# A row mean of 64 MiB: hand-held semaphores, and each load in two halves of 64 partitions on two queues

## The chip, the cores and the metric

The kernel runs on one core of one Trainium2 chip. The metric is the device time of one execution in microseconds (us). The times given are medians of several runs; the profile is of one further execution, taken by the hardware profiler.

## The reference

The input is a 32 x 512 x 1024 array of float32, 64 MiB. Negative elements become zero, and each row of 1024 is averaged:

```python
def reference(x):
    relu_x = np.maximum(x, 0)
    return np.mean(relu_x, axis=-1).astype(np.float32)
```

The output has 32 x 512 float32 elements, 64 KiB.

## The kernel before

The 16,384 rows are spread over the 128 partitions: partition p holds rows p·128 to p·128+127, so J is 128 rows per partition, and each partition's part of the input is contiguous. The kernel walks over J in tiles of NB = 16 rows per partition. A full tile is 128 x 16 x 1024 float32, 8.39 MB, loaded by one DMA that SyncE (SP in the profile) issues on line 97. There are seven full tiles, in a pool of three buffers: the load of tile t+3 goes into the buffer of tile t and so waits until both engines that read tile t are done.

The eighth tile is loaded in pieces that get smaller towards the end, all issued by SyncE: 8, 4, 2 and 1 rows per partition (line 105), and the last row, in a buffer of its own called `last`, in columns of 512, 256 and 256 (line 109).

Each row of a tile is one instruction that takes the maximum with zero and sums along the row. Even rows go to ScalarE (ACT), by `act_row` on line 15; odd rows to VectorE (DVE), by `dve_row` on line 20. Both write over the tile and put the sum into a column of `sums`. GpSimd (POOL) multiplies the sums by 1/1024 into `res` (`finish`, line 90): once for the seven full tiles, once for the first 14 rows of the eighth. The last row but one is shared between ScalarE (448 columns) and VectorE (576), and GpSimd adds both parts (line 121). The last row is shared too: ScalarE sums 512 columns and VectorE 256, into two extra columns of `last`; then one VectorE instruction on line 126 multiplies the remaining 256 columns and those two partial sums by `scale` (filled with 1/1024 on line 81) and sums them into the last column of `res`. SyncE stores `res` by one DMA (line 130).

The order on each engine is the order in which the program is written. A tile framework derives the semaphores and waits from the buffers, hands its semaphores for DMAs out in turn, and on closing (line 134) adds drains, a meeting of all engines, a clear of its semaphores and a second meeting. After that, `issue_ahead_of_entry_barrier` moves SyncE's first load in front of the barrier at the program's entry, which the launching code adds (line 150 in the profile).

Of the kernel before, what the change touches and what calls it, by code (L numbers as in the profile page):

```python
# [1 line left out]

# [4 lines left out]

F32 = mybir.dt.float32
ALU = mybir.AluOpType
ACT = mybir.ActivationFunctionType  # L10


def act_row(nc, src, acc):

    nc.scalar.activation(out=src, in_=src, func=ACT.Relu, accum_out=acc)  # L15


def dve_row(nc, src, acc, init=None):

    nc.vector.tensor_scalar(  # L20
        out=src, in0=src, scalar1=0.0, scalar2=init,
        op0=ALU.max, op1=ALU.add, accum_out=acc,
    )


def issue_ahead_of_entry_barrier(nc):


    entry, body = nc.cur_f.blocks[0].instructions, None
    for block in nc.cur_f.blocks[1:]:  # L30
        for k, ins in enumerate(block.instructions):
            if ins.opcode == "DMACopy":
                body, load = block.instructions, k
                break
        if body is not None:
            break
    first = body[load]
    assert first.engine == mybir.EngineType.SP and not first.sync_info.on_wait
    assert all(i.opcode == "DMACopy" or i.engine != first.engine for i in body[:load])
    del body[load]  # L40
    at = next(k for k, i in enumerate(entry) if i.engine == first.engine and i.opcode == "Drain")
    entry.insert(at, first)


@with_exitstack
def kernel(
    ctx: ExitStack,
    tc: tile.TileContext,
    x: bass.AP,
    out: bass.AP,  # L50
):
    nc = tc.nc
    P = nc.NUM_PARTITIONS
    xf = x.flatten_outer_dims()
    R, D = xf.shape
    assert R % P == 0
    J = R // P
    inv = 1.0 / D
    xr = xf.rearrange("(p j) d -> p j d", p=P, j=J)
    outr = out.flatten().rearrange("(p j) -> p j", p=P, j=J)  # L60
    xlast = xr[:, J - 1, :]

    NB = 16
    full = J // NB - 1

    row_pieces = [8, 4, 2, 1]
    assert sum(row_pieces) == NB - 1
    col_pieces = [512, 256, 256]
    assert sum(col_pieces) == D

    pools = ctx.enter_context(ExitStack())
    in_pool = pools.enter_context(tc.tile_pool(name="in", bufs=3))
    res_pool = pools.enter_context(tc.tile_pool(name="res", bufs=1))
    sums = res_pool.tile([P, J], F32)
    res = res_pool.tile([P, J], F32)
    part = res_pool.tile([P, 2], F32)


    last = res_pool.tile([P, D + 2], F32)
    scale = res_pool.tile([P, D // 4 + 2], F32)  # L80
    nc.gpsimd.memset(scale, inv)  # L81

    def rows(xt, lo, n, j0):

        for k in range(lo, lo + n):
            j = j0 + k
            (dve_row if j % 2 else act_row)(nc, xt[:, k, :], sums[:, j:j + 1])

    def finish(lo, hi):
        nc.gpsimd.tensor_scalar(  # L90
            out=res[:, lo:hi], in0=sums[:, lo:hi], scalar1=inv, scalar2=0.0, op0=ALU.mult, op1=ALU.add,
        )

    for t in range(full):
        j0 = t * NB
        xt = in_pool.tile([P, NB, D], F32, name="xt")
        nc.sync.dma_start(out=xt, in_=xr[:, j0:j0 + NB, :])  # L97
        rows(xt, 0, NB, j0)

    j0 = full * NB  # L100
    xt = in_pool.tile([P, NB, D], F32, name="xt")
    prev = xt[:, NB - 2, :]
    lo = 0
    for n in row_pieces:
        nc.sync.dma_start(out=xt[:, lo:lo + n, :], in_=xr[:, j0 + lo:j0 + lo + n, :])  # L105
        lo += n
    c = 0
    for w in col_pieces:
        nc.sync.dma_start(out=last[:, c:c + w], in_=xlast[:, c:c + w])  # L109
        c += w  # L110

    finish(0, j0)
    lo = 0
    for n in row_pieces[:-1]:
        rows(xt, lo, n, j0)
        lo += n
    finish(j0, j0 + lo)

    act_row(nc, prev[:, :448], part[:, 0:1])
    dve_row(nc, prev[:, 448:], part[:, 1:2])  # L120
    nc.gpsimd.tensor_scalar(  # L121
        out=res[:, J - 2:J - 1], in0=part[:, 0:1], scalar1=part[:, 1:2], scalar2=inv, op0=ALU.add, op1=ALU.mult,
    )
    act_row(nc, last[:, :512], last[:, D:D + 1])
    dve_row(nc, last[:, 512:768], last[:, D + 1:D + 2])
    nc.vector.scalar_tensor_tensor(  # L126
        out=last[:, 768:], in0=last[:, 768:], scalar=0.0, in1=scale, op0=ALU.max, op1=ALU.mult,
        accum_out=res[:, J - 1:J],
    )
    nc.sync.dma_start(out=outr, in_=res)  # L130

    pools.close()
    tc.close()
    tc.compile()  # L134
    issue_ahead_of_entry_barrier(nc)


# [1 line left out]
_INS = ['x']  # L139
_OUTS = [((32, 512), 'float32')]  # L140


# [23 lines left out]
```

## Time and profile before

| | |
|---|---|
| median of 8 runs | 163.72 us (163.32 to 164.02) |
| profiled execution | 163.39 us, of which the span of its instructions is 161.6 us |
| bytes read, written | 67.11 MB, 0.07 MB |
| VectorE busy | 74.3 us |
| ScalarE busy | 69.2 us |
| one row of 1024 on VectorE, on ScalarE | 1208 ns, 1035 ns |

The span runs from the first to the last instruction of the core. "Busy" leaves out the sequencer's work: waits, semaphores and the issue of DMAs; such work has a "q" behind the engine's name (SPq). A line `A <- B: total, times, longest` in a view of waits says how long A waited for B. In the views by window the columns are the stretch, its length, busy time and instructions of VectorE, ScalarE and GpSimd, the granted TensorE clock (not used here), the busy share of 16 DMA engines, and GB/s.

### The profile page before, as it was taken

Reading aid. Unit: us, or ns where it says so; the run is one execution under the profiler, and the core shown is the slowest. Engines: PE = TensorE matmul, PEld = TensorE weight load, DVE = VectorE, ACT = ScalarE, POOL = GpSimd, SP = SyncE. Lnnn points to the kernel's source line nnn. Section 1 sums busy time; section 2 is a strip of 40 time slices with the busy share of each in tenths; the row PEclk is TensorE's granted clock in tenths of the full one; section 3 lists DMA queues with packets and bytes.
Section 4 is the critical chain, followed back from the end, with each engine's and each line's share of the span. In section 5 each row is a group of like instructions: output and inputs, shape, how many; then the busy total and the mean of one; then the engine's idle time right before and its main releaser. Section 6 shows DMA issues by size and latency. Waiting matters only on the chain.

```text
span 161.6 us, 351 instructions
## 1 busy us (share of the span) xinstructions
DVE 74.3 (46%) x132; ACT 69.2 (43%) x131; POOL 1.3 (1%) x8
## 2 busy tenths in 40 slices
DVE  0000049800696008940099202990049800698992
ACT  3000049600694008920099002980049600696882
POOL 1000000000000000000000000000000000000000
DMA  8997997997997997997997998998998996999990
GB/s 308 470 503 308 487 487 324 487 503 324 470 503 308 487 503 308 487 503 308 487 503 328 470 470 357 470 487 357 454 503 357 438 519 300 430 430 406 408 359 21
DMA packets 2162, 67.19 MB, mean 416 GB/s; under 512 B 240, under 2 KB 624, under 8 KB 880
## 3 DMA queue, kind: packets, MB, share of 16 engines
q1 hardware_dynamic: 2160, 67.18, 96.9%
q14 instruction: 2, 0.02, 0.0%
HBM read 67.11 MB, written 0.07 MB: 416 GB/s over the span
## 4 chain that ended last, share of the span: by engine, by line
DMA 84%; DVE 12%; SPq 1%; issue 0%; DVEq 0%
DMA xt<-in_x_dram 56%; DMA last<-in_x_dram 29%; DVE xt L20 11%; SPq L105 1%; SPq L109 0%; DVE last L20 0%; DVE last L126 0%; DVEq L126 0%; DVEq L20 0%; SPq L97 0%; DVEq L134 0%
## 5 line engine op out<-in xcount | busy, mean ns | idle before, releaser
L20 DVE TENSOR_SCALAR_CACHE_REDUCE xt<-xt 128x1024 f32<-128x1024 f32 x64 | 73.4, 1208 | 84.4 <-DMA xt<-in_x_dram 84.0
L15 ACT ACTIVATE xt<-xt 128x1024 f32<-128x1024 f32 x64 | 66.2, 1035 | 88.5 <-DMA xt<-in_x_dram 88.5
L15 ACT ACTIVATION_READ_ACCUMULATOR xt<-xt 128x1 f32 x64 | 11.9, 186 | 0.0
L20 DVE DVE_READ_ACCUMULATOR xt<-xt 128x1 f32 x64 | 5.3, 82 | 0.0
L90 POOL TENSOR_SCALAR res<-sums 128x112 f32<-128x112 f32 (+1 forms) x2 | 0.5, 249 | 155.8 <-DVE xt L20 155.8
L15 ACT ACT_TABLE_LOAD x1 | 1.3, 1283 | 0.8 <-PEq L150 0.8
L15 ACT ACTIVATE last<-last 128x512 f32<-128x512 f32 x1 | 0.6, 630 | 0.0
L126 DVE SCALAR_TENSOR_TENSOR last<-last,scale 128x258 f32<-128x258 f32 x1 | 0.4, 428 | 0.2 <-ACT last L15 0.2
L20 DVE TENSOR_SCALAR_CACHE_REDUCE last<-last 128x256 f32<-128x256 f32 x1 | 0.4, 419 | 0.2 <-DMA last<-in_x_dram 0.2
L81 POOL MEMSET scale<- 128x258 f32 x1 | 0.3, 314 | 0.3 <-POOLq L150 0.3
L121 POOL TENSOR_SCALAR res<-part 128x1 f32<-128x1 f32 x1 | 0.3, 264 | 0.7 <-DVE xt L20 0.7
L15 ACT ACTIVATION_READ_ACCUMULATOR last<-last 128x1 f32 x1 | 0.2, 187 | 0.0
L150 POOL MEMSET const-bfloat16-1.0<- 128x1 bf16 x1 | 0.1, 101 | 0.0
L150 POOL MEMSET const-uint8-127<- 128x1 uint8 x1 | 0.1, 101 | 0.0
L150 POOL MEMSET const-float32-0.0<- 128x1 f32 x1 | 0.1, 98 | 0.2 <-issue 0.2
L150 POOL MEMSET const-float32-1.0<- 128x1 f32 x1 | 0.1, 98 | 0.0
L126 DVE DVE_READ_ACCUMULATOR last<-last,scale 128x1 f32 x1 | 0.1, 83 | 0.0
L20 DVE DVE_READ_ACCUMULATOR last<-last 128x1 f32 x1 | 0.1, 82 | 0.0
## 6 DMA issues: line engine op xcount, KB each, us to landing
xt<-in_x_dram SPq DMA_DIRECT2D x1, 4096.0 KB, 39.0
xt<-in_x_dram SPq DMA_DIRECT2D x1, 2048.0 KB, 43.5
xt<-in_x_dram SPq DMA_DIRECT2D x1, 1024.0 KB, 45.5
xt<-in_x_dram SPq DMA_DIRECT2D x1, 512.0 KB, 46.4
last<-in_x_dram SPq DMA_DIRECT2D x1, 256.0 KB, 46.6
last<-in_x_dram SPq DMA_DIRECT2D x2, 128.0 KB, 42.7
xt<-in_x_dram SPq DMA_DIRECT2D x7, 48.7
out_dram<-res SPq DMA_DIRECT2D x1, 64.0 KB, 1.5
```

What stands on the lines that cost most here:

```text
L15: nc.scalar.activation(out=src, in_=src, func=ACT.Relu, accum_out=acc)
L20: nc.vector.tensor_scalar(out=src, in0=src, scalar1=0.0, scalar2=init, op0=ALU.max, op1=ALU.add, accum_out=acc,)
L81: nc.gpsimd.memset(scale, inv)
L90: nc.gpsimd.tensor_scalar(out=res[:, lo:hi], in0=sums[:, lo:hi], scalar1=inv, scalar2=0.0, op0=ALU.mult, op1=ALU.add,)
L105: nc.sync.dma_start(out=xt[:, lo:lo + n, :], in_=xr[:, j0 + lo:j0 + lo + n, :])
L121: nc.gpsimd.tensor_scalar(out=res[:, J - 2:J - 1], in0=part[:, 0:1], scalar1=part[:, 1:2], scalar2=inv, op0=ALU.add, op1=ALU.mult,)
L126: nc.vector.scalar_tensor_tensor(out=last[:, 768:], in0=last[:, 768:], scalar=0.0, in1=scale, op0=ALU.max, op1=ALU.mult, accum_out=res[:, ...
L150: nc = _bacc.Bacc("TRN2", target_bir_lowering=False, num_devices=1)
```

## The change

The tile context is closed and compiled while it is still empty, at the top of the function. What follows is the same computation with buffers and semaphores of its own:

- Every load has a semaphore `loaded[i]`, and three more count what ScalarE, VectorE and GpSimd have finished. Waits are written out.
- Every load goes in two halves: SyncE issues the one for partitions 0 to 63, ScalarE the one for 64 to 127. Each adds 16 to the load's semaphore, and readers wait for 32. ScalarE issues its first three halves at the start, and the later ones after its rows of the tile whose buffer comes free; both issuers wait until ScalarE and VectorE are done with that tile.
- The first load of each of the two queues is moved in front of the entry barrier.
- At the end only SyncE waits for the store; it clears the other semaphores while the store is under way.

```diff
-    entry, body = nc.cur_f.blocks[0].instructions, None
...
+    for engine in (mybir.EngineType.SP, mybir.EngineType.Activation):
...
+        del body[load]
+        at = next(k for k, i in enumerate(entry) if i.engine == engine and i.opcode == "Drain")
+        entry.insert(at, first)
...
+    tc.close()
+    tc.compile()
...
+    H = P // 2
+
+    def issue(engine, half, t):
+
+        if t >= BUFS:
+            engine.wait_ge(act, t - BUFS + 1)
+            engine.wait_ge(dve, t - BUFS + 1)
+        for i in range(t, t + 1 if t < full else len(loads)):
+            dst, src = loads[i]
+            engine.dma_start(out=dst[half], in_=src[half]).then_inc(loaded[i], 16)
+
+    for t in range(full + 1):
+        issue(nc.sync, slice(0, H), t)
+    for t in range(BUFS):
+        issue(nc.scalar, slice(H, P), t)
...
+    def rows(i, xt, lo, n, j0):
+        nc.scalar.wait_ge(loaded[i], 32)
+        nc.vector.wait_ge(loaded[i], 32)
         for k in range(lo, lo + n):
             j = j0 + k
-            (dve_row if j % 2 else act_row)(nc, xt[:, k, :], sums[:, j:j + 1])
+            done = (dve_row if j % 2 else act_row)(nc, xt[:, k, :], sums[:, j:j + 1])
+            if k >= lo + n - 2:
+                done.then_inc(dve if j % 2 else act, 1)
...
     for t in range(full):
-        j0 = t * NB
-        xt = in_pool.tile([P, NB, D], F32, name="xt")
-        nc.sync.dma_start(out=xt, in_=xr[:, j0:j0 + NB, :])
-        rows(xt, 0, NB, j0)
+        rows(t, bufs[t % BUFS], 0, NB, t * NB)
+        if t + BUFS <= full:
+            issue(nc.scalar, slice(H, P), t + BUFS)
...
+    nc.vector.wait_ge(act, n_done + 1)
+    nc.vector.wait_ge(dve, n_done + 1)
+    nc.vector.wait_ge(loaded[i + 3], 32)
     nc.vector.scalar_tensor_tensor(
...
-    nc.sync.dma_start(out=outr, in_=res)
-
-    pools.close()
-    tc.close()
-    tc.compile()
+    nc.sync.wait_ge(pool, 2)
+    nc.sync.wait_ge(dve, n_done + 2)
+    nc.sync.dma_start(out=outr, in_=res[:, :]).then_inc(stored, 16)
+
+    used = [s.num for s in (*loaded, act, dve, pool)]
+    assert used == list(range(used[0], used[0] + len(used)))
+    nc.sync.sem_clear(range(used[0], used[-1] + 1))
+    nc.sync.wait_ge(stored, 16).then_inc(stored, -16)
```

## The prediction

> **What bounds the kernel now.** I read the page first: busy shares of the engines, the DMA row, the chain that ended last.
>
> ```profile
> span 161.6 us, 351 instructions
> DVE 74.3 (46%) x132; ACT 69.2 (43%) x131; POOL 1.3 (1%) x8
> q1 hardware_dynamic: 2160, 67.18, 96.9%
> HBM read 67.11 MB, written 0.07 MB: 416 GB/s over the span
> DMA 84%; DVE 12%; SPq 1%; issue 0%; DVEq 0%
> ```
>
> No compute engine is busy half the time; the transfer queue is at 96.9%. The chain's 12% on DVE are the first tiles' rows that a reload waits for, with other loads still queued. The stretches between landings, and VectorE's waits in the timeline, give the steady state.
>
> ```profile
> 80.60:100.00 19.40, 9.21 (x16) 8.39 (x16) 0.00 (x0) 1.00 1.00 433
> 100.00:119.40 19.40, 9.21 (x16) 8.45 (x17) 0.00 (x0) 1.00 1.00 432
> 100.06 1.22 DVE L20 TENSOR_SCALAR_CACHE_REDUCE xt<-xt 128x1024 f32<-128x1024 f32 x1 [10.25 <-DMA xt<-in_x_dram]
> 119.41 1.22 DVE L20 TENSOR_SCALAR_CACHE_REDUCE xt<-xt 128x1024 f32<-128x1024 f32 x1 [10.14 <-DMA xt<-in_x_dram]
> ```
>
> A load of 128 x 16 x 1024 x 4 bytes, 8.39 MB, takes 119.41 - 100.06 = 19.35 us: 433.5 GB/s, or 27.1 GB/s for each of 16 DMA engines. VectorE works 9.2 us of it and waits 10.1; ScalarE works 8.4. So the bytes set the time. The first tile is ready at 22.45, so streaming really began at 22.45 - 19.35 = 3.1; the last piece is ready at 158.04. That is 154.9 us of stream, with 3.1 ahead of it and 3.6 behind.
>
> Windows of 0.1 us show single packets (each is credited where it starts):
>
> ```profile
> 6.30:6.40 0.10, 0.00 (x0) 0.00 (x0) 0.00 (x0) 1.00 3.04 1311
> 6.90:7.00 0.10, 0.00 (x0) 0.00 (x0) 0.00 (x0) 1.00 1.51 655
> 7.30:7.40 0.10, 0.00 (x0) 0.00 (x0) 0.00 (x0) 1.00 1.51 655
> 7.40:8.60 1.20, 0.00 (x0) 0.00 (x0) 0.00 (x0) 1.00 0.00 0
> ```
>
> 655 GB/s for 0.1 us is one packet of 65.5 KB, one partition's 16 rows; the share 1.51 of 16 engines is 1.51 x 16 x 0.1 = 2.42 us. The 16 engines start within about 1.0 us (6.3 to 7.4), then nothing starts for 1.2 us: they march in step. This matters below.
>
> SyncE's own waits and line 134, the end of the program:
>
> ```profile
> SPq L109 <- DMA xt<-in_x_dram: 7.2, 1, 7.2
> SPq L134 <- DMA out_dram<-res: 1.0, 1, 1.0
> SPq L134 <- PEq L134: 0.6, 2, 0.4
> L134 SPq DRAIN  x3: 7/7/7, 160.9 to 161.2; - x3
> L134 POOLq EVENT_SEMAPHORE_RANGE_CLEAR  x1: 95/95/95, 161.2 to 161.2; - x1
> ```
>
> After the store has landed, a drain, a meeting of all engines, a semaphore clear and a second meeting fill 160.9 to 161.6.
>
> [...]
>
> **The change, part by part.**
>
> *The end.* What stands from 160.9 to 161.6 goes: 0.7 us off the path. The bounds are 0 (something outside the span waits for the same meeting) and 161.6 - 160.67 = 0.9 (store at 159.17 plus 1.5 to landing). The closing lot of an empty context moves to the start, by these rows 0.7 us; both queues' first loads are ahead of it, and the later ones aren't needed until 22.45, which hides it.
>
> *SyncE.* It issues the same 14 loads at 0.33 to 0.44 us (the first 0.86); with 19 us of bytes queued this costs nothing. The 7.2 us before the last piece on line 109 goes, for nothing too: it ended at 119.3, with 39 us of bytes still queued ahead of that piece.
>
> *ScalarE.* It gains 14 issues. Three at the start, about 2.0 us by SyncE's row, stand before its table load of 1.3 us and are hidden by the first landing. Four times, one issue follows a tile: ScalarE first waits for VectorE to finish (9.2 - 8.4 = 0.8), then issues for 0.4; the rows of the next tile are queued behind. Once seven issues follow, 7 x 0.43 = 3.0. Even 0.8 + 3.0 = 3.8 is under its 10.9 us of idle at a tile. If that cover went, the rows would start late and so would the reload.
>
> *Waits of the compute engines.* Waits are the same but for one more separate wait before line 126, 0.05 us by that line's rows; it can be hidden. GpSimd keeps its order; its clear goes.
>
> *The halves.* This decides. Each engine gets four packets from each queue per tile instead of eight from one; bytes and packet size stay. [...] The starts lie within 1.0 us; two random points in it are a third apart, 0.33 us, f = 0.14: factor 1.86. I see nothing in the trace that drives them apart: at 105.5 to 106.7 us the starts of one round still lie within 1.2 us. The bounds: 2.0 for f = 0, and 1.0 for f = 1[...].
>
> **The sum.** The profiled run took 163.39 (span 161.6 and 1.8 around it), 0.33 below the median 163.72, so the difference is under the last digit I give. 163.39 + 0.86 x 154.9 - 0.7 = 163.39 + 133.2 - 0.7 = 295.9, rounded to 296. With f = 0 it is 317.6[...]. The case's own range, factors 1.75 to 2.0, is 279 to 318.
>
> **The rivals.**
>
> *Faster: the halves run side by side.* [...] 163.39 - 0.7 = 162.7, about 163.0 as a median; 162.5 to 163.3. For it: both queues are always filled two loads ahead, so an engine never lacks the other half's packet. Against it: the march in step[...]. The point from which it decides: stream losses under 0.7 of 154.9 us, 0.45%.
>
> *Partly out of step.* [...]with smaller units the shift is a larger part of a unit[...]. Factors 1.1 to 1.75: 178 to 279.
>
> *A small toll.* [...]a change of queue at each packet costs something the trace can't show, having one queue. At 30 ns on 2.42 us, 1.2%, it is +1.9 - 0.7: 164.6. From 0.5 to 5%: 163.5 to 170.
>
> *Not two queues after all.* If both halves went through one queue, the lower half would finish before the upper starts[...]: factor near 2, in the main case's range.
>
> **How the numbers follow.** In step 0.42; partly 0.18; small toll 0.13; no measurable difference 0.05; side by side 0.22. Slower by over 0.2% is the sum of the first three, 0.73; same 0.05; faster 0.22. About 0.2% is what a measurement of this kernel can tell from no change. The likeliest case gives 296. Cases of both signs are too likely to be left out, so the range is 162.5 to 318; the likeliest one alone has 279 to 318.
>
> **What would show it.** Right: a second hardware queue with half the bytes; about 36 us between landings; DMA near 235 GB/s; packets of 4 to 5 us; compute idle some 27 us a tile; nothing after the store's landing but SyncE's last wait. Wrong: landings 19.4 us apart and packets of 2.42 us, or packets of 4.8 us two at a time on an engine, which is the same rate. Were the span's tail no shorter, the 0.7 would be wrong.

## The result, and the profile after

The changed kernel takes 316.57 us (median of 11 runs, 314.37 to 317.52) where the kernel before takes 163.68 (32 runs): a ratio of 1.9333, with a 95% interval of 1.9305 to 1.9361. The profiled execution took 317.39 us, of which 316.0 are its span. It is slower, and nearly by a factor of two.

From the page after, the same parts as before: busy shares, queues, bytes, the chain by engine.

```profile
span 316.0 us, 355 instructions
DVE 74.3 (24%) x132; ACT 69.2 (22%) x131; POOL 1.3 (0%) x8
q1 hardware_dynamic: 1264, 33.62, 49.4%
q10 hardware_dynamic: 1120, 33.56, 49.3%
HBM read 67.11 MB, written 0.07 MB: 213 GB/s over the span
another core or an unknown queue 62%; DVE 24%; DMA 14%; issue 0%; DVEq 0%
```

The compute engines do the same work, 74.3 and 69.2 us. The bytes are the same, now half on each of two queues, q1 (SyncE's) and q10 (ScalarE's); together they are as busy as the one queue was, and move half as much per microsecond. The chain puts 62% down to "an unknown queue": these pieces lie where VectorE waits for the loads of a tile, whose second half comes by the second queue; the chain doesn't resolve it.

Next come two stretches between landings and VectorE's waits in the timeline. The columns are as before.

```profile
121.90:161.50 39.60, 9.19 (x17) 8.40 (x17) 0.00 (x0) 1.00 1.00 212
161.50:200.80 39.30, 9.19 (x16) 8.40 (x16) 0.00 (x0) 1.00 1.00 213
```
```profile
161.48 1.22 DVE L20 TENSOR_SCALAR_CACHE_REDUCE rows<-rows 128x1024 f32<-128x1024 f32 x1 [30.41 <-DMA rows<-in_x_dram]
200.82 1.22 DVE L20 TENSOR_SCALAR_CACHE_REDUCE rows<-rows 128x1024 f32<-128x1024 f32 x1 [30.14 <-DMA rows<-in_x_dram]
```

A tile lands every 200.82 - 161.48 = 39.3 us, where it took 19.35: 213 GB/s in place of 433. The DMA share is 1.00 in both kernels: the engines are never without a packet, each packet only takes longer. Two windows of the trace after show how much longer:

```profile
21.80:21.90 0.10, 0.00 (x0) 0.00 (x0) 0.00 (x0) 1.00 12.35 2621
26.70:26.80 0.10, 0.00 (x0) 0.00 (x0) 0.00 (x0) 1.00 12.37 2621
```

2621 GB/s for 0.1 us is four packets of 65.5 KB, and 12.35 x 16 x 0.1 / 4 = 4.94 us is the time of each, where it was 2.42.

SyncE's own waits after:

```profile
SPq L109 <- DVE rows L20: 204.7, 5, 49.0
SPq L177 <- DVE last L170: 100.0, 1, 100.0
SPq L183 <- SPq L183: 1.1, 1, 1.1
SPq L55 <- PEq L55: 0.5, 2, 0.3
```

Line 177 is the wait for the last result, line 183 that for the store, and nothing follows it. The meetings of the empty context stand on line 55, at the start. From the issue of the store to the end of the execution it is 317.39 - 314.46 = 2.93 us, where it was 163.39 - 159.17 = 4.22.

### The profile page after: what moved, and what is told of

Read it like the earlier page. It is cut to its first block, busy times and chain, and to the rows that moved or that the text cites. A ratio compares the mean times of both kernels' runs of the same rounds, so it can differ in the third digit from the quotient of the medians.

```text
span 316.0 us, 355 instructions
## 1 busy us (share of the span) xinstructions
DVE 74.3 (24%) x132; ACT 69.2 (22%) x131; POOL 1.3 (0%) x8
## 4 chain that ended last, share of the span: by engine, by line
another core or an unknown queue 62%; DVE 24%; DMA 14%; issue 0%; DVEq 0%
DVE rows L20 23%; DMA rows<-in_x_dram 14%; DVE last L20 0%; DVE last L170 0%; DVEq L169 0%; DVEq L124 0%
## 5 line engine op out<-in xcount | busy, mean ns | idle before, releaser
L20 DVE TENSOR_SCALAR_CACHE_REDUCE rows<-rows 128x1024 f32<-128x1024 f32 x64 | 73.4, 1208 | 239.7 <-DMA rows<-in_x_dram 239.7
L15 ACT ACTIVATE rows<-rows 128x1024 f32<-128x1024 f32 x64 | 66.2, 1035 | 241.0 <-DMA rows<-in_x_dram 241.0
L15 ACT ACTIVATION_READ_ACCUMULATOR rows<-rows 128x1 f32 x64 | 11.9, 187 | 0.0
L20 DVE DVE_READ_ACCUMULATOR rows<-rows 128x1 f32 x64 | 5.3, 83 | 0.0
```

The lines of the kernel that those rows point to most:

```text
L15: return nc.scalar.activation(out=src, in_=src, func=ACT.Relu, accum_out=acc)
L20: return nc.vector.tensor_scalar(out=src, in0=src, scalar1=0.0, scalar2=init, op0=ALU.max, op1=ALU.add, accum_out=acc,)
```

## The experiments

### The semaphores without the halves (sem_whole)

```diff
-    for t in range(full + 1):
-        issue(nc.sync, slice(0, H), t)
-    for t in range(BUFS):
-        issue(nc.scalar, slice(H, P), t)
+    for t in range(full + 1):
+        issue(nc.sync, slice(0, P), t)
...
-        if t + BUFS <= full:
-            issue(nc.scalar, slice(H, P), t + BUFS)
```

Readers wait for 16 where they waited for 32, and only SyncE's first load is moved ahead of the entry barrier.

> The semaphore rewrite alone: whole loads of 128 partitions, all issued by SyncE. Theory[...]: the halves carry the whole loss, so landings stay 19.35 us apart, packets 2.42 us, and only the end gets shorter: 163.7 - 0.7 = 163.0 us, between 162.4 and 163.3. Rival (the rewrite or its waits cost something): above 163.7; if the rewrite carried the loss, near 317.

It took 162.13 us against 163.58 for the kernel before on the same chip, a ratio of 0.9911 (0.9898 to 0.9925). From its timeline:

```profile
100.14 1.22 DVE L20 TENSOR_SCALAR_CACHE_REDUCE rows<-rows 128x1024 f32<-128x1024 f32 x1 [10.16 <-DMA rows<-in_x_dram]
119.50 1.22 DVE L20 TENSOR_SCALAR_CACHE_REDUCE rows<-rows 128x1024 f32<-128x1024 f32 x1 [10.15 <-DMA rows<-in_x_dram]
...
159.24 0.35 SPq L174 DMA_DIRECT2D out_dram<-res  x1
```

The tiles land 19.36 us apart and the store goes out at 159.24, where it went at 159.17. So the stream is untouched, and all that is gained comes after the store. The halves carry the whole loss; the rewrite is a gain, and larger than the 0.7 that was expected: 1.45 us by the medians.

### Two queues, cut by rows (rows_two)

SyncE loads the first half of a tile's rows and ScalarE the second, each on all 128 partitions; the last row is cut by columns.

```diff
+    def cut(odd, ap):
...
+        return ap[:, n // 2:] if odd else ap[:, :n // 2]
...
-            engine.dma_start(out=dst[half], in_=src[half]).then_inc(loaded[i], 16)
+            engine.dma_start(out=cut(odd, dst), in_=cut(odd, src)).then_inc(loaded[i], 16)
...
```

> Two queues as in the changed kernel, but each load is cut by rows (columns for the last row) and not by partitions: SyncE loads rows 0 to 7 of a tile and ScalarE rows 8 to 15, both on all 128 partitions, packets of 32 KB. Theory: [...]alternating between two queues costs nothing: landings 19.4 us apart, 162.5 to 163.7 us in all. Rival (toll of two queues): if alternation is the loss, near 317; a small toll of 1% is 164.6.

163.33 us, ratio 0.9984 (0.9977 to 0.9991), with 431 GB/s between landings:

```profile
100.65:120.10 19.45, 9.22 (x17) 8.44 (x17) 0.00 (x0) 1.00 1.00 431
```

Two queues that alternate don't cost the factor. The time is 1.2 us above that of one queue with the same semaphores (162.13), so a small toll is there. Whose it is this run doesn't tell, since its packets are also half as long, 32 KB (4178 packets in all where the kernel before has 2162); even_odd, below, has two queues and packets of 64 KB.

### The halves on one queue (halves_one)

```diff
...
+            for half in (slice(0, H), slice(H, P)):
+                nc.sync.dma_start(out=dst[half], in_=src[half]).then_inc(loaded[i], 16)
...
```

> The two halves of 64 partitions, both issued by SyncE, one after the other on one queue. Theory: [...]packets of 4.9 us, landings 39.4 us apart, near 317 us. Rival (two queues that alternate are the loss): 19.4 us apart and 163 us.

The one run taken was 328.19 us; two landings from its timeline:

```profile
165.19 1.22 DVE L20 TENSOR_SCALAR_CACHE_REDUCE rows<-rows 128x1024 f32<-128x1024 f32 x1 [31.28 <-DMA rows<-in_x_dram]
205.68 1.22 DVE L20 TENSOR_SCALAR_CACHE_REDUCE rows<-rows 128x1024 f32<-128x1024 f32 x1 [31.28 <-DMA rows<-in_x_dram]
```

With 40.5 us to a tile it is a little slower than on two queues. The second queue isn't the cause. What is left is the halves: that they have 64 partitions, or which 64 these are.

### Single loads: source, destination, count (probe_sets)

Ahead of the kernel of sem_whole, SyncE issues seventeen loads, each after the one before has landed. `far` reads rows as the kernel does, 512 KB apart.

```diff
+    def far(a, b, step=1):
+        return xr[slice(a, b, step), 0:NB, :]
...
+    o, i = probe(slice(0, 64), far(0, 64)); nc.sync.dma_start(out=o, in_=i).then_inc(probed, 16)
...
+    o, i = probe(slice(32, 96), far(0, 64)); nc.sync.dma_start(out=o, in_=i).then_inc(probed, 16)
...
```

> Seventeen single loads of 64 KB per partition from SyncE, each waiting for the one before, ahead of the kernel with whole loads and its own semaphores; they set apart where a load reads (rows 512 KB apart, as in the kernel, or 64 KB apart), where it writes (which partitions) and how many partitions it has. About 2 us of each is fixed. Theory P[...]: what is written decides. 128 partitions 19.4 us + 2; partitions 0 to 63 and 64 to 127, 19.6 + 2 wherever they read; 32 to 95, 9.7 + 2; 32 partitions 9.8 + 2[...]. Theory H (the memory that is read conflicts): the source decides: rows 512 KB apart in partitions 0 to 63 give 19.6 + 2 wherever they are written, and rows 64 KB apart give 9.7 + 2. Theory N (a load of 64 partitions is slow in itself): all of 64 partitions take 19.6 + 2.

SyncE's waits give the time of a load, under the line of the load that waits for it (line 131 waits for the load of line 130, and so on):

```profile
SPq L131 <- DMA rows<-in_x_dram: 22.6, 1, 22.6
SPq L132 <- DMA rows<-in_x_dram: 22.6, 1, 22.6
SPq L133 <- DMA rows<-in_x_dram: 12.4, 1, 12.4
SPq L134 <- DMA rows<-in_x_dram: 22.5, 1, 22.5
SPq L135 <- DMA rows<-in_x_dram: 12.3, 1, 12.3
SPq L136 <- DMA rows<-in_x_dram: 22.5, 1, 22.5
SPq L137 <- DMA rows<-in_x_dram: 11.8, 1, 11.8
SPq L138 <- DMA rows<-in_x_dram: 11.9, 1, 11.9
SPq L139 <- DMA rows<-in_x_dram: 11.8, 1, 11.8
SPq L140 <- DMA rows<-in_x_dram: 4.4, 1, 4.4
SPq L141 <- DMA rows<-in_x_dram: 4.3, 1, 4.3
SPq L142 <- DMA rows<-in_x_dram: 6.7, 1, 6.7
SPq L143 <- DMA rows<-in_x_dram: 10.6, 1, 10.6
```

| line of the load | written partitions | read rows | wait, us |
|---|---|---|---|
| 130 | 0 to 63 | of partitions 0 to 63, 512 KB apart | 22.6 |
| 131 | 64 to 127 | the same | 22.6 |
| 132 | 32 to 95 | the same | 12.4 |
| 133 | 0 to 63 | of partitions 32 to 95, 512 KB apart | 22.5 |
| 134 | 32 to 95 | the same | 12.3 |
| 135 | 0 to 63 | 64 KB apart | 22.5 |
| 136 | 32 to 95 | the same | 11.8 |
| 137 | 0, 2, .., 126 | the same | 11.9 |
| 138 | 0 to 31 (half the bytes) | 64 KB apart | 11.8 |

What is read makes next to no difference (130, 133, 135; 132 and 136 are 0.6 us apart), nor does the count of partitions decide (130 against 132): the set of written partitions does. 0 to 63 takes nearly twice as long as 32 to 95, and as long as all 128 partitions with twice the bytes, which waited 20.9 to 22.1 us (three loads, lines 127 to 129). 0 to 31 with half the bytes takes as long as 32 to 95 with all. The sets of eight partitions, all with the same bytes, differ as well: 4.4 and 4.3 us (0, 4, .., 28 and 64, 68, .., 92), 6.7 (0, 8, .., 56) and 10.6 (0 to 7). The 4.4 less one packet of 2.42 leaves 2.0 us, an estimate of the part that was expected to be fixed. Which part of the hardware makes one set slower than another isn't shown.

### Other halves (even_odd)

```diff
-        issue(nc.sync, slice(0, H), t)
+        issue(nc.sync, slice(0, P, 2), t)
...
-        issue(nc.scalar, slice(H, P), t)
+        issue(nc.scalar, slice(1, P, 2), t)
```

> The changed kernel with one edit: the halves are the even and the odd partitions in place of 0 to 63 and 64 to 127. Two queues, 64 partitions a load, packets of 64 KB and every wait stay. Theory[...] a single load of partitions 0, 2, .., 126 took 12.4 us where 0 to 63 took 23.2, so landings 19.4 us apart and 162.5 to 163.5 us in all. Rival (halves of 64 partitions on two queues are slow together, whatever they reach): near 317.

162.92 us, ratio 0.9955 (0.9939 to 0.9971). Two landings from its timeline:

```profile
100.64 1.22 DVE L20 TENSOR_SCALAR_CACHE_REDUCE rows<-rows 128x1024 f32<-128x1024 f32 x1 [10.15 <-DMA rows<-in_x_dram]
120.01 1.22 DVE L20 TENSOR_SCALAR_CACHE_REDUCE rows<-rows 128x1024 f32<-128x1024 f32 x1 [10.17 <-DMA rows<-in_x_dram]
```

19.37 us to a tile: with the same queues, waits, counts and packets, choosing the halves by parity gives the factor of two back. So the cause is which partitions a half writes, as in the single loads, where 0 to 63 took 22.5 us and every second partition 11.9.

### Half of the engines shifted by a packet (shifted)

By the prediction it saves time when the DMA engines start their packets apart. This kernel shifts half of the engines by a whole packet, with one small load on each queue between the first and the second tile:

```diff
+    def shift(engine, lo):
+        part8, n = slice(H, H + 32, 4), NB // 2
+        engine.dma_start(
+            out=bufs[2][part8, lo:lo + n, :], in_=xr[part8, 2 * NB + lo:2 * NB + lo + n, :],
+        ).then_inc(shifted, 16)
...
```

> The changed kernel with one addition: between the first and the second tile each queue gets one small load of 8 partitions with 32 KB each (rows of tile 2, which tile 2's own loads then write again). It should occupy only half of the 16 DMA engines, and so move those by one packet of 64 KB[...]. Theory with a neutral shift: the first landing interval is 39 us, later ones 19.4; 163 + 20 + 1 for the added 0.5 MB = 184 us.[...] Rival (64-partition loads or two queues are slow in themselves): 318, every interval 39.4.

The one run taken was 321.32 us, where a shift that helps was expected to give 184. The two queues' shares, first in a stretch before the shift, then after it (packets, MB, share of 16 engines; a packet counts where it starts):

```profile
q10 hardware_dynamic: 15, 0.98, 291.9%
```
```profile
q1 hardware_dynamic: 8, 0.52, 145.7%
q10 hardware_dynamic: 8, 0.52, 145.6%
```

Before the shift (35.0 to 36.6 us) the round starts on one queue. After it (55.0 to 56.7) eight engines start on the lower half while eight start on the upper. So the shift took place, and at 252.5 to 254.2 us it is still eight and eight. Yet a packet takes 1.457 x 16 x 1.7 / 8 = 4.95 us as before, and the landings stay 39.4 us apart at the end. That half of the engines are on the other half does not help them.

### Shifts from rest (probe_pairs)

```diff
...
+    # D to G: 8, 4, 2, 1 partitions ahead of the halves on each queue
+    for k in (8, 4, 2, 1):
+        parts = slice(H, H + 4 * k, 4) if k > 1 else slice(H, H + 1)
+        load(nc.sync, 1, parts, 0, 6)
+        load(nc.scalar, 1, parts, 6, 6)
+        load(nc.sync, 2, parts, 0, 6)
+        load(nc.scalar, 2, parts, 6, 6)
+        halves()
+        begin()
...
```

> Loads on both queues at once, in seven groups, each waiting for all loads before it, ahead of the kernel with whole loads and its own semaphores; 64 KB per partition. A: the two halves as in the changed kernel, from rest. B: partitions 32 to 95 on both queues, into two buffers. C: eight partitions of the lower half on SyncE's queue, eight of the upper half on ScalarE's. D to G: the two halves again, behind small loads of 8, 4, 2 and 1 partitions (four of 24 KB each, two on each queue), that keep some DMA engines busy for about one packet and so shift them from the start[...]. Theory 1 ([...]a shift frees them): A 39 us of packets of 4.9 us; B 19.4 us; C 16 packets of 2.4 us; in D, [...]packets of 2.4 us, and in G two of the 16 engines run at 2.4 us[...]. Theory 2 (an engine alternating between the two halves is slow by itself, whatever the others do): C is slow too, 16 packets of 4.9 us, and D to G stay at 4.9 us. Theory 3 (congestion spreads[...]): A and D to G stay at 4.9 us, C is fast.

In A and in D to G the packets took about 4.9 us; in B and C they took 2.42 once under way. A round of G (228.4 to 230.2 us), where one engine was shifted:

```profile
q10 hardware_dynamic: 15, 0.98, 258.1%
q1 hardware_dynamic: 1, 0.07, 17.2%
```

Fifteen engines on one half take 2.581 x 16 x 1.8 / 15 = 4.96 us, and the one on the other half 0.172 x 16 x 1.8 = 4.95, although no other engine starts there. Its last packet, again on the lower half, starts at 259.5 us, when the others have ended (259.4 to 259.6 us):

```profile
q1 hardware_dynamic: 1, 0.07, 76.1%
```

That is 0.761 x 16 x 0.2 = 2.4 us. So it was the work of the other fifteen that slowed it, though they wrote to the other half of the partitions. C, with eight partitions of each half at 2.42 us a packet, excludes that an engine is slow by alternating. This fits the third of the theories named before the run, that congestion spreads. D adds a hint: in its first round, while eight engines still did small loads at 0.91 us for 24 KB, 27.0 GB/s and so the full rate, the other eight already took 4.5 to 5.1 us for a packet of the lower half. Those eight were slow without the shifted eight.

### A bystander (probe_victim)

```diff
+    for parts in (None, slice(0, 8), slice(0, 32, 4)):
+        if parts is not None:
+            load(nc.sync, 0, parts)
...
+        for b in range(BUFS):
+            load(nc.sync if parts is None and b == 0 else nc.scalar, b, slice(40, 96))
+        begin()
```

> Three groups of loads, each from rest, ahead of the kernel with whole loads and its own semaphores. A: three loads of partitions 40 to 95 (56 partitions, which should use 14 DMA engines). B: the same three on ScalarE's queue, beside three loads of partitions 0 to 7 on SyncE's, which use 8 engines[...]. C: the same, the loads beside it on partitions 0, 4, .., 28[...]. Theory 1[...]: the six engines that take no part in the loads beside run at 2.4 us a packet in all groups. Theory 3 (congestion spreads): in B their packets get longer too[...]; in A and C 2.4 us.

First rounds of group B (32.6 to 34.3 us), then a round of group C (96.5 to 97.8):

```profile
q1 hardware_dynamic: 8, 0.52, 246.2%
q10 hardware_dynamic: 6, 0.39, 193.1%
```
```profile
q1 hardware_dynamic: 8, 0.52, 93.6%
q10 hardware_dynamic: 6, 0.39, 69.8%
```

In B eight engines write partitions 0 to 7, at 2.462 x 16 x 1.7 / 8 = 8.4 us a packet. The six engines on the other queue write partitions from 40 to 95, and take 1.931 x 16 x 1.7 / 6 = 8.8 us. The next two times that both queues meet in B, at 47 and 61 us, the six take 8.3 to 9.1 us again. In C the eight write partitions 0, 4, .., 28, and the two groups run at 0.936 x 16 x 1.3 / 8 = 2.43 and 0.698 x 16 x 1.3 / 6 = 2.42 us. So the slow load holds up engines that write other partitions for another queue. By what path isn't shown.

### Smaller packets (halves_pad, whole_pad)

Sixteen bytes between the rows of a buffer make each row of 4 KB a packet of its own, once in the changed kernel and once with whole loads.

```diff
-    bufs = [sbuf(f"rows{b}", P, NB, D) for b in range(BUFS)]
+    bufs = [sbuf(f"rows{b}", P, NB, D + 4) for b in range(BUFS)]
...
```

> The changed kernel with 16 bytes between the rows of a buffer, so that a packet is one row of 4 KB and no longer 16 rows of 64 KB. Theory of the prediction ([...]a shift of fixed time is a larger part of a small packet): faster than 317, factors 1.1 to 1.75, 178 to 279 us. Theory 3[...] with 4 KB turns they may be on both at once, so anything from 165 to 317; at 310 to 330 packet size has no part in it.

> The control for packets of 4 KB: whole loads and own semaphores on one queue, with the same 16 bytes between rows. [...]near the kernel with whole loads: 162 to 166 us, the rest being a toll of small packets. If small packets cost by themselves, above 170.

The one run taken of each was 204.38 and 170.11 us. Landings of the halves, then of the whole loads:

```profile
127.67 1.22 DVE L20 TENSOR_SCALAR_CACHE_REDUCE rows<-rows 128x1024 f32<-128x1024 f32 x1 [15.16 <-DMA rows<-in_x_dram]
152.04 1.22 DVE L20 TENSOR_SCALAR_CACHE_REDUCE rows<-rows 128x1024 f32<-128x1024 f32 x1 [15.17 <-DMA rows<-in_x_dram]
```
```profile
105.24 1.22 DVE L20 TENSOR_SCALAR_CACHE_REDUCE rows<-rows 128x1024 f32<-128x1024 f32 x1 [11.21 <-DMA rows<-in_x_dram]
125.63 1.22 DVE L20 TENSOR_SCALAR_CACHE_REDUCE rows<-rows 128x1024 f32<-128x1024 f32 x1 [11.19 <-DMA rows<-in_x_dram]
```

24.37 us to a tile against 20.39: a factor of 1.20 where packets of 64 KB gave 2.03. With packets of 4 KB the same halves on the same two queues lose far less. From 100 to 110 us of halves_pad both queues start packets in equal number:

```profile
q1 hardware_dynamic: 427, 1.75, 52.4%
q10 hardware_dynamic: 426, 1.68, 50.5%
```

So both halves are written at once. That alone can't be the reason, for in shifted both halves were written at once too, and nothing was gained. Why short packets help stays open, and 204 us lies in the ranges of both theories named before the run. Small packets have a toll of their own, 20.39 against 19.36 us to a tile; 170.11 is above the 162 to 166 that were expected.

## Why the prediction was right or wrong

**The direction and the cause were right.** The likeliest case, halves that lose nearly a factor of two by the partitions they write, is what happened; even_odd, at 162.92 us, and probe_sets, with 22.5 us for 0 to 63 and 11.8 for 32 to 95, show it. Why those partitions are slow together was not shown. The forecast of 296 us missed the measured 316.57 by 20.6, inside the range of that case, 279 to 318, and near its upper end. The whole range, 162.5 to 318, held every case from a small gain to the full factor, so a time inside it says little; that the likeliest case came true is what counts, and it had a chance of 0.42.

**The mis-sized term is the factor 1.86.** The stream now runs from 43.03 - 39.4 = 3.6 us to 313.43, 309.8 us, where it was 154.9. The factor is 2.00, so the halves cost 154.9 us and not 133.2. The step that failed is the shift f = 0.14, the part of a packet by which the starts of two engines were taken to lie apart. That the factor falls from 2.0 to 1.0 as f grows is shown by no run: the spread is still there (in A of probe_pairs the starts of a round lie within 1.8 us), but buys nothing. The time is the one that the prediction gives for f = 0, 317.6 us, yet not because engines in step are what loses: out of step, in shifted, a packet took 4.95. More than the size failed: that a shift saves time did not hold for the shifts that were tried, of eight, four, two and one engines. The shift of one, G of probe_pairs, is the clean test: that engine was on the other half than all the rest, and in the rounds under way all 16 took 4.9 to 5.0 us. The bystander shows the same outcome: beside eight engines at 8.4 us a packet, six that wrote other partitions took 8.8. For the shifts of eight D has the hint of eight engines that were slow, at 4.5 to 5.1 us, while the shifted eight ran at the full rate. Which engines hold each other up in a load of 64 partitions stays open, since the trace doesn't name the engine of a packet.

**The end was right in kind and too small.** 0.7 us was taken off; sem_whole gained 1.45 by the medians. From the store's issue to the end of the span it is 160.8 - 159.24 = 1.6 us where it was 161.6 - 159.17 = 2.4: 0.9, the upper bound of the prediction. Another 0.4 lies outside the span, 162.15 - 160.8 = 1.35 against 163.39 - 161.6 = 1.79. The prediction took the time around the span for fixed. What happens there the profile doesn't show.

**The covers held.** ScalarE's first three issues stretch over 3.4 us and not 2.0, and SyncE's over 3.2, the meetings of the empty context among them; the first landing at 43 us hid them. The seven issues after the fifth tile took about 4.6 us and not 3.0, under 30 us of idle. What was mis-sized is the issue of one load: with 64 partitions it took SyncE 0.47 to 0.60 us, where one of 128 took 0.33 to 0.44, but for the third with its 0.86, which the prediction takes for the first. That both engines issue at once isn't the reason, for in halves_one SyncE issues alone and takes the same 0.47 to 0.60. SyncE's wait of 7.2 us on the last piece is gone and nothing came of it. The meetings, at 1.4 to 2.1 us, lie under the first load.

**The rivals.** Side by side was not the case, and "both queues are always filled" wasn't enough for it. Two halves at once gained 3% over one after the other, 39.3 us to a tile against 40.5 in halves_one. The small toll exists beside the large effect: rows_two and even_odd are 1.2 and 0.8 us above sem_whole. It is hardly one on each change of queue. From the first tile ready to the last piece, sem_whole takes 158.20 - 22.48 = 135.7 us and even_odd, with two queues and packets of 64 KB, 158.79 - 22.93 = 135.9; more than half of its 0.8 lies before the first landing. Only rows_two, with packets of 32 KB, takes 1.0 us longer there, 159.39 - 22.69 = 136.7. Partly out of step, with packets of 4 KB, is the 1.20 of halves_pad. Not two queues after all is excluded by the page after, which has q10, but its time, a factor near 2, is that of halves_one.

With 162.13 us the kernel of sem_whole beats both the kernel before and the changed one.

## What to carry to other kernels

Judge a load by a timing of the partitions it writes, not by how many they are or which queue brings them: here two halves cut at partition 64 took 316.57 us and two halves by parity 162.92. When one part of a change is put on top of another, time each alone; here a gain of 0.9% lay under a loss of 93%. A DMA share of 1.00 says that engines have packets, not that bytes move at the full rate: it stood here beside 433 GB/s and beside 213. Compare the time of one packet of known size, here 2.42 us and 4.94.

## What was not expected of the hardware

- One slow load slows another. Six engines that wrote partitions from 40 to 95 took 8.8 us a packet while eight others wrote partitions 0 to 7 at 8.4, and 2.42 while the eight wrote 0, 4, .., 28 at 2.43.
- The two queues take turns by whole packets of 64 KB, in rounds of all 16 engines. The changed kernel is still in these rounds at 257 us: 16 packets of one queue start within 1.7 us, and 4.9 us later 16 of the other.
- Not every load of 64 partitions is slow: 32 to 95, and every second partition, took 11.8 to 12.4 us where 0 to 63 took 22.5 to 22.6.
- A load of 64 partitions takes longer to issue than one of 128: 0.47 to 0.60 us on SyncE against 0.33 to 0.44 in all but one, whether ScalarE issues beside it (the changed kernel) or not (halves_one).
